# Where the computed instruction order begins: at the decode stretch, or at the input projection

## The chip, the cores and the metric

The kernel runs on one core of one Trainium2 chip. The metric is device time in microseconds (us) of one execution. Five engines work side by side and meet only through semaphores: TensorE (PE, matmul), VectorE (DVE), ScalarE (ACT), GpSimd (POOL) and SyncE (SP, which here only issues DMAs). Each engine works through its own list of instructions in order, so the order that a list is given decides which work stands behind a wait.

## The reference, cut to what matters

The program is one inference step of a hybrid decoder layer for two groups of requests: a prompt of 1024 tokens, and 8 decode requests of 8 tokens each (64 "sample" rows) over 8192 cached tokens.

```python
z = rmsnorm(x, norm_mix_pre) @ w_in                  # (l, 1024) @ (1024, 1056)
c_q, c_kv, k_r, u = z[:256], z[256:512], z[512:544], z[544:]   # by columns
# MLA heads: 8 heads over a latent of 256 and a rotary key of 32
q = rmsnorm(c_q) @ w_uq ; q_lat = q_nope @ w_uk ; s = q_lat.k_lat + q_pe.k_pe
o = softmax(s, causal) @ k_lat ; attn = o @ w_uv     # sample rows: paged cache of 8192 keys
# S5 groups: 32 groups x 16 channels, 64 complex states each
h[t] = A h[t-1] + B u[t] ; y = Re(C h) + D u ; ssm = g * sigmoid(g @ w_glu)
x += rmsnorm(concat(rmsnorm(attn), rmsnorm(ssm)) @ w_out)
x += rmsnorm(cross_attention(x, 256 memory tokens)) ; x += rmsnorm(conv_ffn(x))
```

## The kernel before, in words

The class `Kern` runs its stages one after another: `in` (the input projection), `decopen`, `par` (the decode stretch), `attn` (prompt attention), `mix` (output projection), and then the memory attention and the FFN.

**Input projection (`stage_in`).** The 1024 prompt rows are eight tiles of 128 rows, and the sample rows are a ninth tile of 64 rows, called tile 8, which is worked first: 8, 0, 1, ..., 7. A tile is 72 matmuls at L488: eight chunks k of the 1024 input channels, by three products of a high and a low half (`winh`/`winl` are the halves of the weights, `xh`/`xl` those of the rows), by three column groups of 512, 272 and 272. Each group has a PSUM bank `z`, and there are six banks, so two tiles are under way at once: a tile's matmuls can start only when the tile two before it has been read out of its banks. That is done by ACT (`cz`, L490, the 512 columns) and by DVE: `kr_raw` (L496) and `u_all` (L498, L499) for the two groups of 272. `cn` (L509) is the normalised latent. In the order listings the tiles are told apart by the number in `rs_...`: `rs_595` belongs to tile 3, `rs_798` to tile 4, `rs_1005` to tile 5, `rs_1174` to tile 6, `rs_1344` and `rs_1535` to tile 7. On DVE the stage also prepares the SSM parameters: a chain of small operations that begins with the loaded tile `prm` (`nsgn` L627, `ek` L644, `den` and many lines at L619, L654) and ends in the powers `pw` (L607) and the angles `cs` (L619). Between the tiles of the projection PE turns and multiplies the decode queries (L959 to L995: `wukT`, `qn`, `qnT`, then `Qb`), and turns the SSM input `us` (L749).

**Decode stretch (`stage_par`).** A generator `gen_dec` makes 16 steps of attention over the cache, and after each the next piece of "other" work: the SSM groups, the GLU, and parts of the next stages. A step gathers 1024 rows of the cache (`rf` the rotary keys, `kf` the latents, L1027 on POOL), turns them on DVE (`kT`, L1049, nine transposes of 1024 elements in each of 128 partitions), multiplies them by the queries on PE (`S`, L1060), takes the maximum on DVE (`mx`, L1081), then P on ACT (L1088), PE transposes (L1109) and the output (`ov`, L1125). An SSM group builds `BB`, `W1T`, `big` and `W` on DVE (L619) and uses them on PE (L788, L822, L841, L870, L905).

**What sets the order.** The program order of the stages is not the order in which an engine's list is filled. A scheduler of the framework places the instructions. On top of it the class `Order` fixes a part: from the moment it is made (`Order.__init__` notes the number of instructions so far) to `Order.close()` at the end of the decode stretch, it reads all instructions and their dependences, runs them through a small model of costs (`cost`, `run`), works out a due time for each from the end backwards (`back`), repeats this six times, keeps the order with the smallest modelled total, and pins it for PE, DVE, ACT and POOL by ordering edges. SP's list of DMA issues isn't pinned. In the kernel before, `Order` is made at L1203, in front of the decode stretch, so the model knows only that stretch: in it the gathers and the first `kT` start at time 0, and the input projection, which the scheduler places, isn't there. `Pool` (L45 to L49) is a wrapper for a tile pool; `behind` is the list of pools already closed whose space a new pool may take over, and the model makes a new pool wait for all users of those. Pools of SBUF are opened from the left or the right side (`side`); the pools of the input projection lie on the right.

Of the kernel before, what the change touches and what calls it, by code (L numbers as in the profile page):

```python
# [41 lines left out]
class Pool:  # L42


    def __init__(self, kern, pool, bufs, space, side):  # L45
        self.kern, self.pool, self.bufs = kern, pool, bufs
        self.space, self.open = (space, side), True
        self.behind = [p for p in kern.pools if not p.open and p.space == self.space]
        kern.pools.append(self)  # L49

    def tile(self, shape, dtype, **kw):
# [247 lines left out]
class Kern:  # L299
# [95 lines left out]

    def stage_in(self):
        nc, i, o = self.nc, self.i, self.o
        self.pers = self.pool("pers", 1, self.actx)
        pers = self.pers
        self.u_all = pers.tile([128, 32, 8, 16], F32, tag="u_all", name="u_all")  # L400
# [793 lines left out]
    def stage_par(self):  # L1194

        def side():
            yield from self.ssm_groups
            yield from self.gen_glu()
            yield from self.gen_memkv()
            yield from self.gen_q()  # L1200
            yield from self.gen_attw()

        self.order = Order(self)  # L1203
        other = side()
        for _ in self.gen_dec():
            with self.tc.high_priority(100):
                next(other, None)
        for _ in other:
            pass
        self.order.close()  # L1210
        self.dctx.close()
# [1022 lines left out]
```

## Time and profile before

| what | us |
|---|---|
| median of 3 runs | 1987.0 (1981.37 to 1987.07) |
| the profiled execution, its own time | 1987.95 |
| span of the profiled execution | 1986.1 |
| input projection, first to last matmul of L488 | 8.42 to about 140.5 |
| decode stretch | about 141 to 700 |
| prompt attention | about 700 to 875 |
| output projection to the end | about 875 to 1986 |

One execution was profiled. Times in the rows are microseconds from the start of its span. "Idle before" with an arrow is the time in which the engine stood still in front of an instruction, and what released it. The granted clock is a share of TensorE's full speed of 2.4 GHz; it has two levels, 1.0 and 0.5, and a figure between them is a mean over a stretch. PE is busy for 93% of the span, DVE for 56%.

### The profile page before, as it was taken

Reading aid. Unit: us, or ns where it says so; the run is one execution under the profiler, and the core shown is the slowest. Engines: PE = TensorE matmul, PEld = TensorE weight load, DVE = VectorE, ACT = ScalarE, POOL = GpSimd, SP = SyncE. Lnnn points to the kernel's source line nnn. Section 1 sums busy time; section 2 is a strip of 40 time slices with the busy share of each in tenths; the row PEclk is TensorE's granted clock in tenths of the full one; section 3 lists DMA queues with packets and bytes.
Section 4 is the critical chain, followed back from the end, with each engine's and each line's share of the span. In section 5 each row is a group of like instructions: output and inputs, shape, how many; then the busy total and the mean of one; then the engine's idle time right before and its main releaser. Section 6 shows DMA issues by size and latency. Waiting matters only on the chain.

```text
span 1986.1 us, 31961 instructions
## 1 busy us (share of the span) xinstructions
PE 1846.4 (93%) x12675; PEld 1450.1 (73%) x12675; DVE 1109.6 (56%) x2013; ACT 807.4 (41%) x1598; POOL 514.4 (26%) x550
## 2 busy tenths in 40 slices
PE   8977898789899989999989989999999999999997
PEld 6864445346465578877868868888878999999776
DVE  4359889865646678864255563434544543334433
ACT  5232323234332368764254454333443333333342
POOL 2231111041130024234311023122144421110654
PEclk9887989899899999999999999999999999999999
DMA  7723533453575531231143352333333522222221
GB/s 239 224 72 116 203 113 130 169 214 130 192 271 204 200 94 28 78 137 50 43 138 117 138 191 95 98 101 98 97 105 106 165 86 86 86 85 79 75 85 59
DMA packets 136597, 248.07 MB, mean 125 GB/s; under 512 B 26912, under 2 KB 91232, under 8 KB 132352
## 3 DMA queue, kind: packets, MB, share of 16 engines
q1 hardware_dynamic: 129120, 170.01, 27.2%
q0 software_dynamic: 7328, 76.03, 10.0%
q8 instruction: 100, 1.64, 0.3%
q14 instruction: 49, 0.40, 0.1%
HBM read 217.26 MB, written 27.42 MB: 123 GB/s over the span
## 4 chain that ended last, share of the span: by engine, by line
PE 62%; ACT 2%; DVE 2%; issue 1%; POOL 1%; DMA 1%; SPq 0%; DVEq 0%; ACTq 0%; POOLq 0%
PE ps L2092 26%; PE z L1597 5%; PE ps L335 4%; PE ps L337 4%; PE ps L336 4%; PE b L1752 2%; PE t L1400 1%; PE S L1060 1%; PE ov L1125 1%; PE o L1416 1%; PE o L1417 1%; PE s L1378 1%; PE s L1379 1%; PE s L1380 1%; PE b L335 1%
## 5 line engine op out<-in xcount | busy, mean ns | idle before, releaser
L2092 PE MATMUL ps<-xTl,wh 128*128 128x288 f32 (+1 forms) x1056 | 287.9, 327 | 0.0
L2092 PE MATMUL ps<-xTh,wh 128*128 128x288 f32 (+1 forms) x1056 | 287.7, 327 | 0.0
L2092 PE MATMUL ps<-xTh,wl 128*128 128x288 f32 (+1 forms) x1056 | 287.7, 327 | 0.0
L326 POOL TENSOR_TENSOR wl<-st,wh 128x1024 fp32r<-128x1024 f32 (+1 forms) x52 | 116.7, 2245 | 408.0 <-ACT wh L325 397.7
L326 DVE TENSOR_TENSOR wl<-st,wh 128x1024 fp32r<-128x1024 f32 (+1 forms) x52 | 64.0, 1231 | 249.8 <-ACT wh L325 247.3
L325 ACT ACTIVATE wh<-st 128x1024 fp32r<-128x1024 f32 (+1 forms) x104 | 102.6, 993 | 235.4 <-PE ps L2092 215.2
L2092 PEld LDWEIGHTS ps<-xTl,wh 128*128 128x128 f32 x1056 | 179.6, 188 | 13.9
L2092 PEld LDWEIGHTS ps<-xTh,wl 128*128 128x128 f32 x1056 | 179.5, 188 | 13.8
L2092 PEld LDWEIGHTS ps<-xTh,wh 128*128 128x128 f32 x1056 | 179.6, 188 | 13.7
L1060 PE MATMUL S<-kT,Qb 32*64 32x512 f32 x2304 | 163.1, 641 | 27.0 <-DVE kT L1049 20.3
L326 DVE TENSOR_TENSOR wdl<-std,wdh 128x1024 fp32r<-128x1024 f32 x44 | 100.4, 2282 | 147.3 <-ACT wdh L325 147.3
L1049 DVE STREAM_TRANSPOSE kT<-kf 128x1024 f32<-128x1024 f32 x128 | 152.4, 1222 | 32.5 <-DMA kf<-in_cache_kv_dram,idx 22.9
L2043 POOL TENSOR_TENSOR al<-act,ah 128x1024 fp32r<-128x1024 f32 x44 | 106.8, 2428 | 174.0 <-ACT ah L2042 174.0
L335 PE MATMUL ps<-wdh,ah 128*128 128x512 f32 x352 | 139.5, 396 | 0.0
L336 PE MATMUL ps<-wdl,ah 128*128 128x512 f32 x352 | 139.1, 395 | 0.0
L1125 PE MATMUL ov<-kf,PT 128*64 128x256 f32 x1024 | 126.6, 394 | 0.7 <-ACT PT L1110 0.7
L337 PE MATMUL ps<-wdh,al 128*128 128x512 f32 x352 | 126.1, 396 | 0.0
L1125 PEld LDWEIGHTS ov<-kf,PT 128*64 128x64 f32 x1024 | 70.6, 141 | 54.6 <-issue 15.1
L1060 PEld LDWEIGHTS S<-kT,Qb 32*64 32x64 f32 x2304 | 46.6, 136 | 84.8 <-issue 40.0
L2042 ACT ACTIVATE ah<-act 128x1024 fp32r<-128x1024 f32 (+1 forms) x44 | 49.0, 1113 | 142.1 <-PE ps L336 136.9
L335 PEld LDWEIGHTS ps<-wdh,ah 128*128 128x128 f32 x352 | 66.2, 188 | 17.4 <-issue 0.8
L1027 POOL DMA_INDIRECT kf<-in_cache_kv_dram,idx x32 | 33.3, 1040 | 175.1 <-PE ov L1125 169.3
(536 smaller groups left out, 3945.9 us busy)
## 6 DMA issues: line engine op xcount, KB each, us to landing
st<-in_w_gate_dram SPq DMA_DIRECT2D x22, 1024.0 KB
st<-in_w_up_dram SPq DMA_DIRECT2D x22, 1024.0 KB
std<-in_w_down_dram SPq DMA_DIRECT2D x44, 512.0 KB
x<-in_x_prompt_dram SPq DMA_DIRECT2D x16, 512.0 KB
x<-x2d SPq DMA_DIRECT2D x15, 512.0 KB
wst<-in_w_in_dram SPq DMA_DIRECT2D x8, 528.0 KB
xT<-in_xT_dram SPq DMA_DIRECT2D x8, 512.0 KB
ws<-in_w_out_dram SPq DMA_DIRECT2D x8, 512.0 KB
```

Of the source, the lines that this page charges most:

```text
L325: nc.scalar.activation(hi, src, AF.Copy)
L326: (lo_eng or nc.vector).tensor_sub(lo, src, hi.bitcast(F32))
L335: mm(ps, lh, rh, start=start, stop=False)
L336: mm(ps, lh, rl, start=False, stop=False)
L337: mm(ps, ll, rh, start=False, stop=stop)
L1049: V.transpose(t, RF[n] if kb == 8 else KF[n][:, :, :, kb * 32:kb * 32 + 32])
L1060: nc.tensor.matmul(SS[n][half[a], j], Qb[q, kb, 2 * p + a], ts[q, a], start=kb == BLOCKS[0], stop=kb == BLOCKS[-1])
L1125: nc.tensor.matmul(ov[half[a]], PTS[n, g][:, m, half[a]], KF[n][:, a, g * 4 + m], start=g == 0 and m == 0, stop=g == 3 and m == 3)
L1597: nc.tensor.matmul(z[n], l, r[:, n * 512:(n + 1) * 512], start=a, stop=b)
L2042: nc.scalar.activation(ah[:, :, :nt], a[:, :, :nt], AF.Copy)
L2043: G.tensor_sub(al, a[:, :, :512], ah[:, :, :512].bitcast(F32))
L2092: nc.tensor.matmul(zt[:, :c1 - c0], l[:, k], r[:, k, c0:c1], start=a, stop=b)
```

## The change

Two lines. `Order` is made at the beginning of `stage_in` and no longer in `stage_par`, so that the instructions of the input projection are in the modelled and pinned part. And `Pool.behind` takes every closed pool in the same memory (`space[0]`), on whichever side it lay, where it took only those of the same side. Line numbers from 398 to 1203 of the changed kernel are larger by one.

```diff
@@ -45,7 +45,7 @@ class Pool, __init__
         self.space, self.open = (space, side), True
-        self.behind = [p for p in kern.pools if not p.open and p.space == self.space]
+        self.behind = [p for p in kern.pools if not p.open and p.space[0] == self.space[0]]
         kern.pools.append(self)
@@ -395,6 +395,7 @@ class Kern
     def stage_in(self):
         nc, i, o = self.nc, self.i, self.o
+        self.order = Order(self)
         self.pers = self.pool("pers", 1, self.actx)
@@ -1200,7 +1201,6 @@ class Kern, stage_par
-        self.order = Order(self)
         other = side()
         for _ in self.gen_dec():
```

The amount of work on each engine stays the same; what moves is its order. Three places follow.

The first is DVE's list in the middle of the input projection, at the head of the SSM parameter chain. Before:

```order
L738 MEMSET cs_1301 128x32
L627 TENSOR_SCALAR nsgn<-prm 128x1
L644 TENSOR_SCALAR ek<-prm 128x32
L619 TENSOR_TENSOR den<-prm 128x32
...
L654 TENSOR_SCALAR ey<-ey 128x32
L496 TENSOR_SCALAR kr_raw<-z,rs_595 128x32
L498 TENSOR_SCALAR u_all<-z,rs_595 128x15x16
L499 TENSOR_SCALAR u_all<-z,rs_595 128x17x16
```

The same place in the changed kernel:

```order
L739 MEMSET cs_1301 128x32
L497 TENSOR_SCALAR kr_raw<-z,rs_595 128x32
L499 TENSOR_SCALAR u_all<-z,rs_595 128x15x16
L500 TENSOR_SCALAR u_all<-z,rs_595 128x17x16
L326 TENSOR_TENSOR xl<-xT,xh 128x512 x2
L510 SCALAR_TENSOR_TENSOR cn<-cz,rs_886,b_kv_norm 128x256
L645 TENSOR_SCALAR ek<-prm 128x32
```

Tile 3 is now read out, and the rows of a later tile split, ahead of the first operation on `prm`.

The second place is the end of that chain, where tile 5 is read out. Before:

```order
L607 TENSOR_TENSOR pw<-pt_1136 128x128
L723 COPY p_1297<-pw 128x32
L619 TENSOR_TENSOR pt_1136<-cs_1301,ph 128x64
...
L619 TENSOR_TENSOR cs_1301<-pt_1136,pt_1137 128x32x4 x2
L496 TENSOR_SCALAR kr_raw<-z,rs_1005 128x32
L498 TENSOR_SCALAR u_all<-z,rs_1005 128x15x16
L499 TENSOR_SCALAR u_all<-z,rs_1005 128x17x16
```

In the changed kernel:

```order
L608 TENSOR_TENSOR pw<-pt_1136 128x128
L497 TENSOR_SCALAR kr_raw<-z,rs_1005 128x32
L499 TENSOR_SCALAR u_all<-z,rs_1005 128x15x16
L500 TENSOR_SCALAR u_all<-z,rs_1005 128x17x16
L326 TENSOR_TENSOR xl<-xT,xh 128x512 x2
L620 TENSOR_TENSOR pt_1136<-cs_1301,ph 128x64
```

The reading of tile 5 stands ahead of the angles `cs` and no longer behind them.

The third place is DVE's list where the input projection ends and the decode stretch begins. Before:

```order
L496 TENSOR_SCALAR kr_raw<-z,rs_1344 128x32
L498 TENSOR_SCALAR u_all<-z,rs_1344 128x15x16
L499 TENSOR_SCALAR u_all<-z,rs_1344 128x17x16
L509 SCALAR_TENSOR_TENSOR cn<-cz,rs_1535,b_kv_norm 128x256
L835 TENSOR_TENSOR kd<-ident,ssd 16x64
L619 TENSOR_TENSOR BB<-bc,f 128x128
...
L619 TENSOR_TENSOR W_1658<-Cst,pw 128x576
L1049 STREAM_TRANSPOSE kT<-rf 128x1024
```

In the changed kernel:

```order
L510 SCALAR_TENSOR_TENSOR cn<-cz,rs_1535,b_kv_norm 128x256
L497 TENSOR_SCALAR kr_raw<-z,rs_1344 128x32
L499 TENSOR_SCALAR u_all<-z,rs_1344 128x15x16
L500 TENSOR_SCALAR u_all<-z,rs_1344 128x17x16
L1050 STREAM_TRANSPOSE kT<-rf 128x1024
L1050 STREAM_TRANSPOSE kT<-kf 128x1024 x2
L620 TENSOR_TENSOR BB<-bc,f 128x128
```

`cn` is done ahead of the last reading of `z`, and the transposes `kT` of the first attention step follow directly, where the first SSM group stood. On PE, the 72 matmuls of tile 8 are drawn together at the front of the list: the last group of tile 8, which needs chunk 7 of `winl`, has about 91 matmuls ahead of it, where tile 8's groups were spread among those of the next tiles. In the last tile the matmuls of the 512-column group come first and those of the 272-column groups last.

## Rows read from the trace of the kernel before

**Rows 1.** The page, busy time, share of span and count of each engine:
```profile
PE 1846.4 (93%) x12675; PEld 1450.1 (73%) x12675; DVE 1109.6 (56%) x2013; ACT 807.4 (41%) x1598; POOL 514.4 (26%) x550
```

**Rows 2.** By stretch: PE, PEld, DVE, ACT, POOL busy; PE clock, DMA share, GB/s:
```profile
8.40:61.70 53.30, 53.07 (x320) 45.09 (x321) 27.08 (x47) 30.16 (x53) 16.01 (x39) 1.00 0.76 239
61.70:71.60 9.90, 5.08 (x45) 4.77 (x44) 3.31 (x6) 5.48 (x14) 4.51 (x12) 0.67 0.99 380
112.60:123.50 10.90, 4.77 (x20) 4.58 (x20) 7.50 (x28) 3.54 (x9) 5.59 (x14) 0.69 0.05 17
140.50:166.00 25.50, 13.02 (x100) 9.80 (x99) 20.70 (x54) 5.83 (x17) 8.39 (x15) 0.56 0.66 231
145.00:410.00 265.00, 218.10 (x2296) 118.31 (x2296) 235.75 (x455) 73.24 (x204) 36.80 (x42) 0.87 0.42 150
410.00:700.00 290.00, 263.11 (x2499) 157.02 (x2500) 175.22 (x275) 105.85 (x238) 55.29 (x51) 0.96 0.56 199
```

**Rows 3.** Timeline of PE: start, duration, operation, idle before and releaser:
```profile
66.82 0.69 PE L981 MATMUL z<-qnT,wukT 64*128 64x64 f32 x2 [4.82 <-DVE qnT L971]
...
118.73 0.57 PE L488 MATMUL z<-winh,xh 128*128 128x272 f32 x1 [6.13 <-DVE u_all L498]
119.09 0.43 PE L488 MATMUL z<-winl,xh 128*128 128x272 f32 x1
119.31 0.43 PE L488 MATMUL z<-winh,xl 128*128 128x272 f32 x1
...
123.98 0.65 PE L488 MATMUL z<-winh,xl 128*128 128x512 f32 x3
124.47 0.64 PE L488 MATMUL z<-winh,xh 128*128 128x512 f32 x3
...
149.07 1.98 PE L1060 MATMUL S<-kT,Qb 32*64 32x512 f32 x11 [7.25 <-DVE kT L1049]
```

**Rows 4.** Timeline of DVE in the input projection:
```profile
27.36 1.32 DVE L331 SCALAR_TENSOR_TENSOR winl<-wst,cols,winh 128x1056 fp32r<-128x1056 f32 x1 [1.75 <-ACT winh L330]
...
65.15 0.68 DVE L326 TENSOR_TENSOR xl<-xT,xh 128x512 fp32r<-128x512 f32 x1
...
66.35 0.42 DVE L971 COPY qnT<-z 128x256 f32<-128x256 f32 x1
...
92.00 0.15 DVE L627 TENSOR_SCALAR nsgn<-prm 128x1 f32<-128x1 f32 x1 [19.85 <-DMA prm<-in_ssm_par_dram]
...
95.10 0.25 DVE L496 TENSOR_SCALAR kr_raw<-z,rs 128x32 f32<-128x32 f32 x1
...
96.15 1.39 DVE L326 TENSOR_TENSOR xl<-xT,xh 128x512 fp32r<-128x512 f32 x2
...
113.73 0.43 DVE L607 TENSOR_TENSOR pw<-pt 128x128 f32<-128x128 f32 x1
...
118.50 0.49 DVE L499 TENSOR_SCALAR u_all<-z,rs 128x272 f32<-128x272 f32 x1
```

**Rows 5.** Timeline of SP, the issue of the SSM parameters:
```profile
81.56 0.65 SPq L625 DMA_DIRECT2D prm<-in_ssm_par_dram  x1
```

**Rows 6.** Timeline of DVE from the last projection tile on:
```profile
140.96 0.49 DVE L499 TENSOR_SCALAR u_all<-z,rs 128x272 f32<-128x272 f32 x1
...
144.96 0.29 DVE L619 TENSOR_TENSOR BB<-bc,f 128x128 f32<-128x128 f32 x1 [1.19 <-DMA bc<-in_ssm_bc_dram]
...
164.71 9.10 DVE L1049 STREAM_TRANSPOSE kT<-kf 128x1024 f32<-128x1024 f32 x8
...
176.38 2.29 DVE L1081 TENSOR_REDUCE mx<-S 128x1 f32<-128x2048 f32 x1
...
270.54 2.29 DVE L1081 TENSOR_REDUCE mx<-S 128x1 f32<-128x2048 f32 x1 [4.67 <-PE S L1060]
```

**Rows 7.** Timeline of POOL, the last gather issued for the first step:
```profile
62.26 0.94 POOL L1027 DMA_INDIRECT kf<-in_cache_kv_dram,idx  x1 [0.30 <-issue]
```

**Rows 8.** Waits of DVE from 145 to 410 (sum, times, longest):
```profile
DVE mx L1081 <- PE S L1060: 11.0, 3, 4.7
```

## The prediction

> **What bounds the kernel now.** I read the page's busy times first, then busy time by stretch, then the timelines of PE and DVE at the stretches that stand out, and last the sums of waits. PE is busy for 1846.4 of 1986.1 us [rows 1], so over the whole span little is to be had. The reader is to see by stretch where the rest lies [rows 2]. In the first weights' stretch, 8.4 to 61.7, PE is full at clock 1.00. In 61.7 to 71.6 it works 5.08 of 9.9 us at 0.67, in 112.6 to 123.5 4.77 of 10.9 at 0.69, and from 140.5 to 166 13.02 of 25.5 at 0.56. From 145 to 410 DVE is the fuller engine (235.75 of 265 us, so 29.25 idle, against PE's 218.10), and from 410 to 700 it is PE again (263.11 of 290).
>
> The timelines say what PE stands for in the three holes [rows 3]: 4.82 us for `qnT`, 6.13 us for a `u_all` that frees a bank of `z`, and 7.25 us for the first `kT`. All three are released by DVE, and in all three DVE works on something else at the time. `qnT` stands behind an `xl` of 0.68 us and others [rows 4]. The `u_all` of tile 5 stands behind the SSM parameter chain, which itself begins at 92.00 after 19.85 us of standing for `prm` [rows 4]. `kT` of `kf` begins at 164.71 [rows 6], though its gather was issued at 62.26 [rows 7].
>
> **The change part by part.** No work is added: the instructions are the same, and the sum is over waits. The edit of `Pool.behind` only adds orderings to the model, and I give it no term: it has none on the chip by itself.
>
> *Tile 8 first.* Its last group needs chunk 7 of `winl`, done at 27.36 + 1.32 = 28.68 [rows 4]. Three warm matmuls take 0.48 us (123.98 to 124.47, [rows 3]), 0.16 each, so the 91 matmuls ahead of that group would be through at 8.42 + 14.6 = 23.0. The cost lies between 0 (the front is paced by arriving weights as before, and nothing is added) and 5.7 (28.68 - 23.0); I take 2.6, near the middle, since some waits for earlier chunks already lie in it.
>
> *`qnT`.* In the new list one `xl` that stood ahead of `qnT` stands behind it, and `u_all` and `wukT` are earlier. `qnT` ended at 66.77; an operation of 0.68 and about as much of queue goes, so about 65.2. PE comes 2.6 us later, at about 64.4, and waits some 0.7 instead of 4.8. After that its work to the next tile takes as long as before (66.82 to 71.6, 4.8 us), so it ends at about 70.2: 1.4 earlier. Bounds: 0 (the `xl` is itself late) to 3 (tile 8 costs nothing).
>
> *Tile 5's bank.* `prm` is issued at 81.56 [rows 5] behind the query loads, which hang on this piece of PE's work, and it arrives when `nsgn` starts, 92.00; I move both by the 1.4, to 90.6. From 92.00 to the end of `pw` takes 113.73 + 0.43 - 92.00 = 22.16. Out of it go what now stands ahead of `prm`, in idle time: tile 3's reading (from 95.10 on, about 1.0), two `xl` (1.39) and a `cn`, which I put at the 0.5 of a `u_all`; 19.3 are left. So `pw` ends at 109.9, and the `u_all` directly behind it frees the bank some 0.7 later, at 110.6; before, PE went on at 118.73 [rows 3]. PE reaches that bank about 1.4 earlier than 112.6, but the last tiles' groups stand in another order, so I let it come to it sooner, at about 106.4; it waits about 4.2 instead of 6.1. 70 matmuls remain of that tile: 70 x 0.16 = 11.2, and 2 for a start at the half clock, to 123.8; the last tile takes 72 x 0.16 = 11.5, to about 135.3 instead of 140.4. In-stage sum: -5.1. Bounds: -2 (the chain gains only its 1.4 and a little) to -9 (the hole closes entirely: 1.4 + 6.1 + about 2 of clock).
>
> The row on the clock: after the hole PE's matmuls of 272 columns start 0.22 us apart (119.09 to 119.31), and later three with a 512 among them take 0.48 [rows 3]; the stretch stands at 0.69, a mix of the levels 1.2 and 2.4 GHz [rows 2]. The Trainium skill's "TensorE: Matmul & The Clock Gate" (Part 1: The HAM clock gate) says that idleness throttles PE to half its clock and that sustained work releases it. This case's trace agrees (0.67 and 0.69 behind two holes, 1.00 before them). By that rule a hole of 0.7 us would leave the clock up and a hole of 4.2 might, which would give another 2 us at each place; the sum above goes without it, by the slow piece of 2 us kept.
>
> *The first step of the decode stretch.* Before, DVE ends `u_all` at 141.45 and goes without a pause only from 144.96 on, where `BB` has waited for a DMA [rows 6]. After, `kT` of the rotary keys and two of the latents follow `u_all` directly, and their data have been there since long before [rows 7]. DVE's stream of work thus begins about 1.2 us behind PE's last projection matmul instead of 4.56 (144.96 - 140.4): -3.2, bounds -1.5 (the memory of `kT` is freed late by a store) to -3.4. `BB` stands three transposes of 1.2 us later, time for its `bc` to land.
>
> *The rest.* `kT` x8 stood at 164.71, the first `mx` at 176.38 [rows 6]; both come some 15 to 20 us sooner, and the SSM group that stood there later. That is an exchange on DVE, which is the fuller engine up to 410 and has the same work: the stretch moves by its start, and PE's gain there isn't the end. How the interleaving after it changes DVE's 29.25 us of idleness [rows 2] can't be read from before; I take 0, bounds +5 and -5 (about a sixth of it), and PE's part from 410 moves with it.
>
> Sum: -5.1 - 3.2 + 0 = -8.3. The profiled execution took 1987.95 us (span 1986.1), so 1979.65; it lies 0.95 above the median of 1987.0, and against that I predict 1978.7.
>
> **The rivals.** *Given back.* The projection gains 2 to 3 us, or the decode stretch swallows the early start: DVE is idle there for 29.25 us already, and if idleness grows by 4 to 8 us the sum is -5 to 0. For it: `mx` waits for PE's scores 11.0 us in three places [rows 8], and such a wait ends with PE, not with DVE's list. Against it: PE starts sooner as well. Time: 1982 to 1987.
>
> *More than that.* The clock stays up behind both holes (-2 each) and the earlier scores take away part of the idleness of DVE (-5): -8.3 - 9 = -17.3, to about 1970. For it: PE's 7.25 us and the half clock in 140.5 to 166 (0.56, [rows 2]) go, so the scores of the first steps are ready earlier. Against it: from 145 on DVE's work, not the scores, is the limit.
>
> *Slower.* With the first step's transposes drawn together, DVE has less SSM work left to put between the transposes and the `mx` of the same step, and each `mx` waits for PE's last scores as the one at 270.54 does, 4.67 us [rows 6]. Eight steps lie in 145 to 410: 8 x 4.67 = 37.4, against 11.0 now [rows 8], +26.4. With -8.3 that is +18.1, to 2005; half of it gives +4.9. It decides from the point at which those waits sum to over 11.0 + 8.3 = 19.3. Against it: five of eight steps don't wait now, with the same work per step.
>
> *It doesn't do what it says.* That the order is pinned on from the projection is plain in the new lists, so this is not left, save that SP isn't pinned: a `prm` that is issued later would undo about the -5.1, and is counted with the first rival.
>
> **How the numbers follow.** The forecast (-5 to -13) 0.47, given back 0.28, more 0.12, slower 0.13. A difference below 0.3%, 6 us, can't be told from none in this kernel. Of the forecast's own range, 1974 to 1982, the part below 1981 is faster: nearly all, 0.45; with the larger gain 0.57. Of "given back", and the remainder of the forecast, 0.30 is same; half of "slower" stays under 6 us, which adds little: 0.31 same, 0.12 slower. The range that leaves out 2 in 10 goes from 1968, the larger gain, to 1989, the first tenth of the slower case.
>
> **What would show it.** In the changed profile: PE's wait for `qnT` under 1.5 us; tile 3's `u_all` before `prm` lands, at about 84; tile 5's `u_all` at about 110 and PE's wait for it at most 5; the last projection matmul near 135; the first `kT` about 1 us behind it, and the first `mx` some 20 us sooner. The hs and `mx` rows around 410 should come 8 to 9 us sooner, and everything behind 700 by the same. It is wrong if PE's last projection matmul comes later than 139, if DVE's idleness between the projection and the eighth step exceeds 38 us, or if PE's waits behind 410 grow.

## The result, and the profile after

The changed kernel takes 1966.15 us (median of 6, 1962.64 to 1969.26), the kernel before, run beside it, 1985.15 (1979.34 to 1991.38): ratio 0.9897, interval 0.9881 to 0.9913, that is -20.4 us (the two medians lie 19.0 apart). The forecast was -8.3 us (1978.7, range 1968 to 1989). The direction was right; the gain is more than twice as large. The profiled execution of the changed kernel took 1969.26 us, span 1967.5.

By stretch, in the columns of [rows 2] and its windows up to 410, the changed kernel reads:

```profile
8.40:61.70 53.30, 49.26 (x271) 40.46 (x270) 24.64 (x42) 28.95 (x52) 13.82 (x36) 0.94 0.68 216
61.70:71.60 9.90, 9.04 (x85) 8.23 (x84) 4.86 (x11) 5.09 (x12) 7.14 (x14) 1.00 0.92 332
112.60:123.50 10.90, 9.94 (x54) 9.04 (x55) 9.54 (x46) 0.93 (x3) 7.06 (x18) 0.76 0.02 5
140.50:166.00 25.50, 17.74 (x218) 7.12 (x218) 25.02 (x48) 7.96 (x21) 6.71 (x7) 0.86 0.65 228
145.00:410.00 265.00, 231.61 (x2490) 124.12 (x2491) 248.05 (x476) 86.65 (x231) 54.13 (x51) 0.90 0.45 165
```

The first stretch has become worse (49.26 busy of 53.3, clock 0.94), the other holes of the projection are smaller or have moved, and from 145 to 410 DVE is busy for 248.05 us instead of 235.75. The line of 145 to 410 carries the result.

PE's timeline, answering to [rows 3]:

```profile
69.44 2.27 PE L982 MATMUL z<-qnT,wukT 64*128 64x64 f32 x29 [0.86 <-DVE qnT L972]
...
113.56 1.03 PE L750 MATMUL z<-ident,us 32*128 32x32 f32 x8 [6.10 <-DVE ey L655]
...
116.45 1.08 PE L489 MATMUL z<-winh,xl 128*128 128x512 f32 x3
...
118.03 0.64 PE L489 MATMUL z<-winl,xh 128*128 128x512 f32 x3
```

The wait for `qnT` is down from 4.82 to 0.86 us and the 6.13 us in the middle of tile 6 are gone, but 6.10 us now stand ahead of the turning of `us`. The row names `ey` as what ended that wait; what PE needs there is the load of `us`, issued at 111.26:

```profile
111.26 0.32 SPq L687 DMA_DIRECT2D us<-usd  x1
```

DVE, answering to [rows 4, 6]:

```profile
84.28 0.25 DVE L497 TENSOR_SCALAR kr_raw<-z,rs 128x32 f32<-128x32 f32 x1 [11.61 <-PE z L489]
...
98.83 0.18 DVE L645 TENSOR_SCALAR ek<-prm 128x32 f32<-128x32 f32 x1 [9.85 <-DMA prm<-in_ssm_par_dram]
...
118.87 0.24 DVE L497 TENSOR_SCALAR kr_raw<-z,rs 128x32 f32<-128x32 f32 x1
...
139.41 0.50 DVE L500 TENSOR_SCALAR u_all<-z,rs 128x272 f32<-128x272 f32 x1 [0.37 <-PE z L489]
139.83 1.24 DVE L1050 STREAM_TRANSPOSE kT<-rf 128x1024 f32<-128x1024 f32 x1
...
157.50 2.27 DVE L1082 TENSOR_REDUCE mx<-S 128x1 f32<-128x2048 f32 x1
```

Tile 3 is read at 84.28 ahead of `prm`, and `kT` follows the last `u_all` without a gap, both as the lists say. But `prm` came at 98.83, 6.8 us later than before. Of this, 5.6 us are its issue on SP (87.14, where it was 81.56 [rows 5]). It stands behind the query loads `Qb`, which read back what the store `qld` has written and so wait for its landing. They were issued 7.7 us after it before, and are 11.7 us after it now. Before:

```profile
71.97 0.37 SPq L985 DMA_DIRECT2D qld<-Ql  x1
79.66 1.80 SPq L987 DMA_DIRECT2D Qb<-qld  x4
```

In the changed kernel:

```profile
73.26 0.39 SPq L986 DMA_DIRECT2D qld<-Ql  x1
84.98 2.06 SPq L988 DMA_DIRECT2D Qb<-qld  x4
87.14 0.59 SPq L626 DMA_DIRECT2D prm<-in_ssm_par_dram  x1
```

The four gathers of the first step are also issued 4.2 us later (62.38 to 66.44 us, where it was 58.20 to 62.26), and their queue moves 1.88 MB between the store and the query loads, where it moved 0.93. That the store lands later because it shares the DMA engines with more of the gathers fits this, but no run shows it by itself.

To see where the 18.7 us between the two profiled executions lie, three pieces are enough: from the start to the last `u_all`; from there to the last `mx` (the decode stretch); and from there to the last L2092 (the FFN's up projections). The second piece of before and after, by stretch (columns as in [rows 2]):

```profile
141.50:678.30 536.80, 463.81 (x4649) 263.52 (x4649) 399.74 (x702) 171.41 (x426) 94.29 (x100) 0.92 0.49 176
```

```profile
139.90:649.10 509.20, 456.34 (x4635) 257.56 (x4635) 395.26 (x703) 169.83 (x420) 98.31 (x95) 0.92 0.51 184
```

The projection gives -1.6 us (139.9 against 141.5), the decode stretch -27.6 (509.2 against 536.8; PE idles 52.9 us in it instead of 73.0, and is busy for 7.5 us less), and what lies behind takes back 10.7 (1161.7 against 1151.0). DVE is the fuller engine up to the first `g` of the GLU. From the last `u_all` to that `g`, before (141.5 to 432.6), it waits for scores 11.0 us ahead of `mx`, the same as in [rows 8], and 9.0 ahead of `kT`:

```profile
DVE kT L1049 <- PE S L1060: 9.0, 6, 5.3
```

After (139.9 to 401.0):

```profile
DVE kT L1050 <- PE S L1061: 6.9, 4, 2.3
DVE mx L1082 <- PE S L1061: 1.7, 2, 1.4
```

The 11.0 us of `mx` have become 1.7. In the same stretch DVE idles 16.9 us of 261.1, where it idled 39.5 of 291.1 before. The waits for scores are about half of that difference; the rest is spread over small waits. Besides, 7.4 us of DVE's work that stood ahead of `g` now stand behind it (251.6 us busy before, 244.2 after).

### The profile page after: what moved, and what is told of

Same layout as the page of the kernel before. It is cut to its first block, busy times and chain, and to the rows that moved or that the text cites. A ratio compares the mean times of both kernels' runs of the same rounds, so it can differ in the third digit from the quotient of the medians.

```text
span 1967.5 us, 31959 instructions
## 1 busy us (share of the span) xinstructions
PE 1849.1 (94%) x12675; PEld 1450.0 (74%) x12675; DVE 1104.5 (56%) x2013; ACT 806.7 (41%) x1598; POOL 520.2 (26%) x550
## 4 chain that ended last, share of the span: by engine, by line
PE 62%; DVE 3%; issue 3%; DMA 3%; ACT 3%; POOL 1%; SPq 0%; DVEq 0%; ACTq 0%; POOLq 0%
PE ps L2092 27%; PE z L1597 5%; PE ps L335 4%; PE ps L337 4%; PE ps L336 4%; PE b L1752 2%; DMA kf<-in_cache_kv_dram,idx 1%; PE t L1400 1%; PE ov L1126 1%; PE S L1061 1%; PE o L1417 1%; PE s L1378 1%; PE o L1416 1%; PE s L1379 1%; PE s L1380 1%
## 5 line engine op out<-in xcount | busy, mean ns | idle before, releaser
L2092 PE MATMUL ps<-xTh,wh 128*128 128x288 f32 (+1 forms) x1056 | 289.2, 328 | 2.4 <-DVE pt L1487 2.4
L2092 PE MATMUL ps<-xTl,wh 128*128 128x288 f32 (+1 forms) x1056 | 289.1, 328 | 0.0
L2092 PE MATMUL ps<-xTh,wl 128*128 128x288 f32 (+1 forms) x1056 | 288.6, 328 | 0.0
L2092 PEld LDWEIGHTS ps<-xTh,wh 128*128 128x128 f32 x1056 | 180.2, 189 | 16.9 <-issue 2.8
L2092 PEld LDWEIGHTS ps<-xTh,wl 128*128 128x128 f32 x1056 | 180.2, 189 | 14.1
L2092 PEld LDWEIGHTS ps<-xTl,wh 128*128 128x128 f32 x1056 | 180.3, 189 | 13.8
L1061 PE MATMUL S<-kT,Qb 32*64 32x512 f32 x2304 | 156.6, 642 | 14.3 <-DVE kT L1050 8.4
L1126 PE MATMUL ov<-kf,PT 128*64 128x256 f32 x1024 | 132.0, 406 | 0.6 <-ACT PT L1111 0.6
L2042 ACT ACTIVATE ah<-act 128x1024 fp32r<-128x1024 f32 (+1 forms) x44 | 49.0, 1113 | 141.8 <-PE ps L336 141.5
L1061 PEld LDWEIGHTS S<-kT,Qb 32*64 32x64 f32 x2304 | 42.2, 137 | 66.9 <-issue 33.5
L335 PEld LDWEIGHTS ps<-wdh,ah 128*128 128x128 f32 x352 | 66.2, 188 | 17.3 <-issue 0.8
```

The source lines that it names most:

```text
L335: mm(ps, lh, rh, start=start, stop=False)
L1061: nc.tensor.matmul(SS[n][half[a], j], Qb[q, kb, 2 * p + a], ts[q, a], start=kb == BLOCKS[0], stop=kb == BLOCKS[-1])
L1126: nc.tensor.matmul(ov[half[a]], PTS[n, g][:, m, half[a]], KF[n][:, a, g * 4 + m], start=g == 0 and m == 0, stop=g == 3 and m == 3)
L2042: nc.scalar.activation(ah[:, :, :nt], a[:, :, :nt], AF.Copy)
L2092: nc.tensor.matmul(zt[:, :c1 - c0], l[:, k], r[:, k, c0:c1], start=a, stop=b)
```

## The experiments

Two theories were set against each other: A, the gain is the recomputed order inside the decode stretch; B, it is the projection's own new order, which ends sooner and feeds the decode stretch. Ratios are to the kernel before, timed on the same chip (medians of before there: 1994 to 1995 us; 1985 for the changed kernel's own row). The last three columns are of the one profiled execution of each run: the end of the last `u_all`, from there to the start of the last `mx`, and from there to the last L2092.

| run | ratio (interval) | last `u_all` ends | to last `mx` | to last L2092 |
|---|---|---|---|---|
| before (profiled) | | 141.5 | 536.8 | 1151.0 |
| changed (profiled) | 0.9897 (0.9881 to 0.9913) | 139.9 | 509.2 | 1161.7 |
| e1 changed again | 0.9886 (0.9866 to 0.9906) | 138.6 | 517.7 | 1160.7 |
| e2 decode order only | 0.9924 (0.9899 to 0.9949) | 143.7 | 523.5 | 1158.2 |
| e3 projection order only | 0.9962 (0.9940 to 0.9984) | 134.3 | 535.1 | 1151.9 |
| e4 gathers there at start | 0.9943 (0.9924 to 0.9963) | 141.0 | 522.7 | 1157.7 |
| e5 before again | none, one run of 1994.0 us | 141.9 | 540.8 | 1152.7 |
| e6 head only | 0.9991 (0.9964 to 1.0017) | 141.1 | 543.9 | 1151.0 |
| e7 changed, prm early | 0.9844 (0.9820 to 0.9868) | 132.6 | 512.6 | 1154.8 |
| e8 before, prm early | 0.9937 (0.9913 to 0.9961) | 133.4 | 542.1 | 1151.2 |
| e9 changed, prm pool only | 0.9846 (0.9816 to 0.9876) | 133.5 | 515.8 | 1154.2 |
| e10 e2, prm early | 0.9879 (0.9851 to 0.9907) | 132.4 | 515.1 | 1157.7 |
| e11 e7 again | 0.9828 (0.9796 to 0.9860) | 129.8 | 517.4 | 1156.1 |

**e1, the changed kernel again.** 

> The changed kernel once more, to see how much of its trace repeats. Profiled before: last matmul of the projection near 139.4 us, first mx 157.5, GLU's first g 401.0, prompt attention from 673.6, FFN (L2092) from 1161.0, span 1967.5; against before, 18.9 us ahead at the first mx, 31.5 at g, but only 20.7 at the FFN and 18.6 at the end. Both theories (order inside the decode stretch; early end of the projection) expect the same numbers here within 2 us and a ratio of 0.990. If the 8 us that are lost between 967 and 1161 are chance, they move by several us; if they belong to the order, the FFN begins at 1161 within 1.5 us again.

The trace repeats the three pieces within 9 us: the decode stretch took 517.7, and behind it 1160.7, so that the loss there is no chance of one execution (it moved by 1 us). The FFN began at 1167.4, not at 1161, and that comes out of the decode stretch, which one trace gives only to some 9 us. DVE's waits there repeat for `mx` (0.3 us) and not for `kT` (12.2). The ratio agrees.

**e2, only the decode stretch pinned.**
```diff
-        order = {e: [tr[k] for k in v] for e, v in best[1].items()}
+        order = {e: [tr[k] for k in v if k >= self.mark(tr)] for e, v in best[1].items()}
```
(`mark` is the number of modelled instructions ahead of the decode stretch.) 

> Order is made at the projection as in the changed kernel and models all of it, but only the decode stretch is pinned to the result; the projection is left to the scheduler as before. Theory A (the gain is the decode stretch's new order, which the model finds because in its time the first gathers are there when the stretch begins): the decode stretch keeps its gain of 25 to 30 us from its start to g, and the projection ends at about 140 as before, or 1 us later: 1960 to 1970 us, ratio about 0.990. Theory B (the gain comes from the projection's own new order, which ends earlier and feeds the decode stretch sooner): the gain goes with it, 1980 to 1986 us. Theory C (the pinned projection costs time at tile 8 and at prm, 6 us each, which its other moves win back): faster than the changed kernel by 0 to 5 us.

The decode stretch keeps the gain (523.5), the projection doesn't (143.7), and 0.9924 is two thirds of the whole. That is theory A for the most part. Theory C, that pinning the projection costs time, falls: e2 is slower than the changed kernel.

**e3, only the projection pinned** to the new order, the decode stretch with an `Order` of its own as before.
```diff
-        self.order = Order(self)
+        self.order_in = Order(self, True)
...
-        order = {e: [tr[k] for k in v] for e, v in best[1].items()}
+        order = {e: [tr[k] for k in v if (k < self.mark(tr)) == self.head] for e, v in best[1].items()}
...
+        self.order = Order(self)
         other = side()
```


> The complement: the projection is pinned to the order of the changed kernel, the decode stretch is ordered by a second Order made where before made it, with its pool rule. Theory A: the gain goes, the sum is that of the projection alone, -1 to -2 us: 1982 to 1987 us. Theory B: the gain stays, 1963 to 1972 us. By my prediction's steps (projection -5.1, of which the trace of the changed kernel shows about -1): 1980 to 1984.

0.9962, the remaining third; 0.9924 and 0.9962 together make 0.9886, what e1 measured. The third is some 7 us, more than the 1 to 2 of theory A's forecast. The decode stretch is at 535.1 as before. In the profiled execution, one of the fastest of the twelve (1979.9 us, median 1987.5), the projection ended at 134.3, 4 to 6 us sooner than with the same pinned order in e1 and the changed kernel. What differs is how late `prm` came: 95.0 here, 97.0 in e1, 98.8 in the changed kernel, and PE's wait ahead of `us` was 1.9, 3.8 and 6.1 us.

**e4, before, with the first gathers done at the model's time 0.**
```diff
-        work = []
+        work, gathers = [], 0
...
+            if type(x).__name__ == "InstDMACopy" and eng[k] == "Pool" and gathers < 4:
+                gathers, busy, end = gathers + 1, 1.0, 1.0
```


> The kernel before, with Order where it was and the pool rule as it was; only the model's costs differ: the four gathers of the first step count as done at the model's time 0. Theory A (what the model has to know is only that these gathers are past): the decode stretch gets nearly the order of the changed kernel, and gains as much: 1960 to 1970 us, DVE idle between its first decode work and g about 17 us where it was 36.6. Theory B: no gain, 1983 to 1988. If the gain needed the projection in the model for another reason (its banks and memory), it would lie between.

Two lines in the model's costs give the decode stretch the changed kernel's list on DVE and PE, but for a few rows, nearly all of them at its head, and the length of e2 (522.7). This kernel has the old pool rule, so the other line of the change isn't needed for that list. So what the model gained from beginning at the projection is one fact for the decode stretch: that the keys of the first step are there. The ratio, 0.9943, is e2's within the intervals. DVE's idleness up to `g` is 25.9 us; I had expected 17. Over all traces the decode stretch takes 509.2 to 523.5 us with the new list and 535.1 to 543.9 with the old one.

**e5, before again.** 

> The kernel before, once more, for a trace from the same chip as the next ones. All theories: last reading of u_all near 141, first mx near 176, g near 432, FFN (L2092) from about 1182.

541 us of decode stretch and 1152.7 behind it; the numbers of before are no single case.

**e6, only the head moved.**
```diff
+        for e, first, count in (("DVE", "kT", 9), ("PE", "S", 72)):
+            out = lambda x: x.outs[0].bass_ap.tensor.name.split("_")[0]
+            v = order[e]
+            head = [x for x in v if out(x) == first][:count]
+            at = 4 if e == "PE" else 0
+            rest = [x for x in v if x not in head]
+            order[e] = rest[:at] + head + rest[at:]
```


> The kernel before with one thing moved by hand: after its order is computed, the nine transposes kT of the first attention step go to the front of DVE's decode list and their 72 score matmuls behind the first four matmuls of PE's; everything else keeps its order. Theory A1 (the gain is that head: attention gets one step ahead of the SSM groups and stays there, so that DVE no longer stands for scores): first mx near 160, DVE's idleness up to g down from 36.6 to about 17, gain 10 to 15 us like the other kernels with a new decode order, 0.993. Theory A2 (the gain lies in the whole recomputed order, step by step): DVE's idleness stays above 28, the SSM work is merely pushed back by 11 us, and the time is within 5 us of before, 0.998 to 1.002.

No gain: 0.9991, decode stretch 543.9. `kT` of `kf` came at 144.4, 20 us sooner than before, and still DVE stood for scores as before (here from 141.1 to 431.8; this kernel's lines stand seven further down):

```profile
DVE mx L1088 <- PE S L1067: 11.4, 3, 4.9
DVE kT L1056 <- PE S L1067: 10.3, 7, 4.7
```

It is not the early transposes and scores by themselves: theory A2. The `mx` of that step kept its place in DVE's list and came at 172.8, 4 us sooner and not near 160, so a head that takes the `mx` along wasn't run. What brings the gain in e2 and e4 is the whole recomputed order.

**e7 and e8, prm loaded in tile 1 of the projection,** into a pool that lives longer, in the changed kernel and in the one before.
```diff
             if t == 1:
+                self.prm = self.pers.tile([128, 4, 32], F32, name="prm")
+                nc.sync.dma_start(self.prm, i["ssm_par"])
...
-        prm = new(c2, "prm", [128, 4, 32])
-        nc.sync.dma_start(prm, i["ssm_par"])
+        prm = self.prm
```


> The changed kernel with prm in a memory of its own, loaded in tile 1 of the projection, ahead of the query loads on SP's queue. In its traces prm is used at 97.0 to 98.8 (before: 92.0), and the chain behind it releases us, for which PE then waits 3.8 to 6.1 us ahead of tile 6 and falls to the half clock. Theory P (prm's arrival sets the end of the projection in the changed order): the chain starts at about 89, behind tile 3's readings; the wait at L749 goes, the last projection matmul comes at 130 to 133 instead of 137.7 to 139.1, and the whole gains 4 to 7 us more, ratio to before 0.985 to 0.987. Rival: another store or load on the same path (xT, usd) is as late, and nothing moves.

> The same early load of prm in the kernel before: nothing else is edited, its orders are computed as before. By my prediction's step on tile 5's bank, the wait of 19.85 us for prm at 92.0 is what holds tile 5's reading back by 6.1 us: with prm there at about 75 the chain ends some 10 us sooner, PE's wait of 6.13 us and the half clock behind it go, and the projection ends at 132 to 134 instead of 140: 0.9955 to 0.997 if the decode stretch passes that on. Rival: the scheduler orders the chain by other costs and the wait moves to us or to another bank: no change beyond 3 us.

Both projections end at about 133. In e7 PE doesn't stand at all from 100 to 131.8, at full clock (columns as in [rows 2]):

```profile
100.00:131.80 31.80, 31.80 (x203) 28.78 (x201) 13.87 (x55) 8.56 (x23) 12.15 (x34) 1.00 0.20 70
```

`prm`'s arrival is what held the end of the projection, in either order: theory P. In the kernel before that alone ends the projection 8 us sooner, and the decode stretch passes it on: by its interval the ratio is a gain of 8 to 17 us, more than the forecast 0.9955 to 0.997. In the changed one the time fell by some 8 us (0.9886 to 0.9844), and the part behind the last `mx` was shorter too (1154.8 us against 1160.7 in e1), which led to the next run.

**e9, only the pool of prm changed,** in the changed kernel.
```diff
-        prm = new(c2, "prm", [128, 4, 32])
+        prm = self.pers.tile([128, 4, 32], F32, name="prm")
```


> The changed kernel with prm in the longer-lived pool as in e7, but loaded where it was, behind the query loads. Two things are told apart with it. The lists of PE behind the decode stretch come in two versions only: before, e3, e6, e7, e8 have the one (tail 1), the changed kernel, e2 and e4 the other (tail 2); this kernel has tail 1. Theory T (tail 2 costs the time that the changed kernel loses between the output projection and the end): from the last mx to the first L2092 it takes 503 to 506 us and L2092 647.6 to 649.5, not 508 to 512 and 649.7, so 6 to 8 us less than the changed kernel; ratio 0.984 to 0.987 if the projection ends at 137 to 139 as there, since the early load of prm is missing. Rival (e7's gain came all from the early prm): like the changed kernel, 0.9886.

This run didn't tell apart what it was meant to. The load stayed where it was in the code, but SP issued it at 8.47:

```profile
8.47 0.33 SPq L626 DMA_DIRECT2D prm<-in_ssm_par_dram  x1
```

So it was the memory, and not the place in the program, that had held the load behind the query loads, and e9 is e7 once more (0.9846). In e7 the load was issued at 8.73.

**e10, e2 with prm early, and e11, e7 again;** the edits are those of e2 and e7.

> e2 (only the decode stretch pinned to the new order, projection left to the scheduler) with prm loaded early as in e7; it has tail 2. By the sum of the parts: the projection ends at 131 to 133 instead of 142.1 (e2), so 8 to 10 us better than e2's 0.9924: 0.987 to 0.989; and behind the last mx it loses to e7 again 6 to 8 us, by theory T. Rival: the tails cost the same, and it comes out equal to e7, 0.984 to 0.985.

> e7 again on the chip of e9 and e10, for the comparison and to confirm that it beats both kernels: 0.982 to 0.987 of before, projection ended at 131 to 133, first mx at 150, 4 to 7 us below e9 by the early prm alone.

e10 gains on e2 what the projection gains (143.7 to 132.4), and its ratio is as forecast. With `prm` early the projection ends at 132.4 where the scheduler orders it and at 129.8 to 133.5 where it is pinned (e7, e9, e11), so that pinning it has nothing clear left to win. e11 is not below e9 (medians 1963.9 and 1962.0), since e9 had its `prm` early too. Against e9 and e11, e10 takes 2 to 4 us longer behind the decode stretch. Over all traces, what follows the last `mx` takes 1151.0 to 1152.7 with the old decode order; 1154.2 to 1156.1 with the new one and, from the output projection on, the same list of PE as before (e7, e9, e11); and 1157.7 to 1161.7 with the new one and the other list (changed, e1, e2, e4, e10). The edit doesn't order that list: it differs from within the output projection on, in the order of the memory attention above all. So some 3 us of the loss go with the new decode order and some 4 with the list that the scheduler lays behind it; no run changed either alone. Theory T had the direction, with 6 to 8 for the list alone. e7, e9 and e11 are the fastest version, 1.5 to 1.7% below before.

## Why the prediction was wrong, by its steps

- **Tile 8 first, +2.6 us:** under-sized. PE's standing for `winh` and `winl` behind its first matmul is of the forecast size (4.0 us in the changed kernel, 2.7 in e1, 0.2 before). But around these waits the granted clock falls, to 0.63 from 28 to 32 us and 0.52 from 32 to 36 (1.00 before), and the term had no clock in it. The 288 matmuls of the first four tiles, with the eight turnings of `wuk` that follow or lie among them, end at 67.7 us, in e1 at 65.2, and ended at 61.6: 6.1 and 3.6 us later. The first is above the upper bound of 5.7.
- **`qnT`:** the wait was forecast at 0.7 us and is 0.86 (1.41 in e1), but by luck. `qnT` was to end at 65.2 and PE to come at 64.4; in the changed kernel it ends at 69.4 and PE comes at 68.6. The clock, which the sum left out, gives half of this back: the stretch from 61.7 to 71.6 stands at 1.00 where it was 0.67, and the work on the queries up to the next tile takes 2.7 us where it took 4.8. Behind the 6.10 us ahead of `us` the granted clock is 0.52 from 113.5 to 118.0, where three matmuls take 0.88 us (116.45 to 117.33), and 1.00 from there to the end of the projection (three take 0.48 from 118.03). The Trainium skill's "TensorE: Matmul & The Clock Gate" (Part 1: The HAM clock gate) says that idleness throttles PE and that activity releases the throttle; these rows agree.
- **Tile 5's bank, in-stage sum -5.1:** wrong in this kernel. The last projection matmul ends at 139.4, 1.1 us sooner than before (2.5 in e1); the forecast was 135.3. I moved `prm` 1.4 us ahead with PE's work on the queries; it came 6.8 us later, since its place behind the query loads on SP follows the landing of `qld`, not PE. The prediction had named a `prm` that is issued later, but only among the rivals. So tile 5 was read at 118.87, not near 110. And the wait went from the bank to `us`, which is loaded into the memory of `wide` (the same tag in the code), a tile of the same chain; the prediction didn't name that one. With `prm` early the last projection matmul ends at 132.0 (e7).
- **First step of the decode stretch, -3.2:** right. The gap from 141.45 to 144.96 is gone, 3.5 us; `kT` begins at 139.83, 0.45 us behind PE's last projection matmul.
- **The rest, 0 within 5 on either side:** this is the step that failed. Net of the gap it is -24.1 us in the decode stretch and +10.7 behind it in the profiled pair; e1 against e5, -23.1 with the gap, and +8.0. I took the recomputed list for an exchange on DVE that moves the old stretch by its start, and bounded the rest by a sixth of DVE's idleness. In the window of that bound, 145 to 410, the idleness fell by 12.3 us (29.25 to 16.95), where I had allowed 5. Up to `g` the new list takes away about half of it (39.5 to 16.9 us, 23.5 in e1), and of PE's 73.0 us of idleness in the stretch 20 (52.9; 63.4 in e1). The slower rival had the right place, the `mx` that waits for scores, and the wrong sign.
- **The "more" rival** (-17.3, chance 0.12) is nearest to the result, by one of the two mechanisms it named: DVE's idleness, at -5 where it was -16 to -22.6. Of its two holes, behind which the clock was to stay up, only that of `qnT` closed.

What stays open: which of the many small moves inside the decode stretch makes the `mx` wait go. e6 excludes the early transposes and scores of the first step; e2 and e4 show that the whole list does it; single steps weren't moved apart. Whether the pool line matters for the projection's order is open too; for the decode list it doesn't (e4). Why the part behind the decode stretch is longer with the new order isn't shown.

## What to carry to other kernels

When an order is computed, ask what its model believes at time 0: here, data that had landed long ago counted as on the way, and the whole list behind was built around it; two lines that say so bring half of the gain or more. A recomputed list can't be priced by where it begins and by its equal work; count the waits that the old one has at its hottest place, and let the range go to all of them. And the wait that the reorder was to remove hung on one late load here: look at what the load's memory waits for; freeing it was worth 0.6% here (e8), the new decode order 0.8% (e2).

## What the runs showed that I had not expected

A list that the edit doesn't pin changed with it: the scheduler's order of the memory attention, behind the whole decode stretch and the prompt attention, came out in one of two versions, and one of them goes with some 4 us more of 1155. And the kernel before took 1985 us beside the changed kernel and 1994 to 1995 in all the later runs, 0.5% apart, so that only ratios to runs taken side by side can be compared.
